# One tile for a raw weight piece and its block sums, and weight pools by stage, in a two-layer mLSTM and attention trunk

## The chip, the cores and the metric

The kernel runs on one core of a Trainium2 chip, in one launch. The metric is the device time in microseconds (us). Before the change the median of 3 runs is 2645.78 us (2642.27 to 2648.69).

## The reference

512 positions of width 2048 go through two layers, all in float32. Each layer normalises, scales and shifts its input by values computed from a condition vector c, and adds a gated branch to the residual stream. The first layer's branch is an mLSTM of 8 heads, the second's an attention of 16 heads in a band of chunks with a learned bias; the second reads keys and values computed from the residual stream after the first.

```
proj = h @ w_in                      # layer 1: 2048 -> q, k (8 x 256), v, o, z (8 x 512), gates
qk = silu(causal_conv(q, k))
ht = rmsnorm_per_head(mlstm(q, k, v, li, lf))
x  = x + gate * rmsnorm((sigmoid(o) * ht * silu(z)) @ w_out)

kv = modulate(rmsnorm(x)) @ kv_w     # keys and values, 2048 each
qz = h2 @ w_in                       # layer 2: q and z, 2048 each
o  = softmax(q k^T / sqrt(128) + bias, band) v
x  = x + gate * rmsnorm((o * silu(z)) @ w_out)
```

## The kernel before, in words

Every float32 product is made of three products of a faster form. `split` (line 244) makes two halves of a tile: ScalarE (ACT) casts it to the rounded form, `hi`, and VectorE (DVE) subtracts this from the source, `lo`. `mm3` issues hi x hi, hi x lo and lo x hi on TensorE (PE). All products have line 316.

Weights come in pieces. A piece is a raw tile `wr` of 128 x 1024 numbers (512 KB), loaded by a DMA on SyncE's queue (SP, line 260, `raw_load`) from a stream `wst` that lies in the order of use; `wpiece` splits it into the halves of a tile `wh`. Where a stage saves multiplications by sums of weight blocks (`proj_s` and `proj_v`: late heads, keys, attention's queries), `wpiece` first makes block sums: three DVE operations (lines 283, 284, 285) write a tile `ws` of 128 x 768, one of them over a block of the raw tile, and `ws` is split by a cast and a subtraction of its own into a tile `wsh`. PE uses `wh` and `wsh` in turn: of the four banks d, c, a, b of a product, d and b need `wh`, c needs `wsh`, a needs both.

One pool `wp`, opened at the start and never closed, holds the raw tiles (3 buffers) and the `wh` tiles (3 buffers). Tiles `ws` and `wsh` (2 buffers each) lie in pools of the stages. A tile of 2 x 1024 halves has 128 spare numbers, and the two halves start at offsets in it that `WIDE`, `STILL` and `MOVING` give by kind of stage.

The stages, in order: modulation sums (tiles `ada`, 1 MB loads of the condition's weights, summed on DVE at line 555) beside the products of head 0 and 1; head 2, whose v still uses whole weights; late heads 3 to 7 (q, k, v, o, z with block sums, 32 pieces each); the first layer's output projection (`ps_y`); values and keys; attention (16 heads of 4 pieces); the second output projection. Line 1301 copies values out of the banks, line 1302 stores them to a scratch `vsc`; line 1016 stores a head's gated output `zo` to the scratch `ysc`, from where the output projection loads it.

A scheduler sets the order on each engine. Each engine's queue is worked in order, SP's too: a load that waits holds up those behind it. Tiles of a pool that is opened where others lay wait, tile by tile, for the last use of what lay there (`reuse_waits="tile"`).

Of the kernel before, what the change touches and what calls it, by code (L numbers as in the profile page):

```python
# [9 lines left out]
F32 = mybir.dt.float32  # L10
F32R = mybir.dt.float32r
# [4 lines left out]
P = 128  # L16
D = 2048
S = 512
# [14 lines left out]
EXTW = 640  # L33
AHEAD = 300
RAW_BUFS = 3
SPARE = 128
WIDE, STILL, MOVING = (64, 0, 64, 1), (16, 0, 48, 1), (28, 0, 28, 1)

PAIRS = [(0, 1), (2, 3)]
BLOCKS = [(0, 2), (2, 6), (6, 12), (12, 16)]  # L40
# [149 lines left out]
def hybrid_trunk(ctx, tc, xT, xN, c, adaT, cols, wst, wg, ext, kc, out):  # L190
    nc = tc.nc
# [59 lines left out]
    loads = []  # L251
    pin = tc.keep_in_program_order

    def raw_load(keep=lambda ins: ins):

        i, at = wpos
        n = sum(w for _, _, w in order[i][1])
        wpos[:] = i + 1, at + P * n
        raw = wp.tile([P, 1024], F32, tag="raw", name=f"wr{i}", bufs=RAW_BUFS)[:, :n]
        keep(nc.sync.dma_start(raw, wst[at : at + P * n].rearrange("(p n) -> p n", p=P)))  # L260
        loads.append(raw)

    def wpiece(mat, groups=(), pl=None, bufs=(2, 2), early=False, at=WIDE):
# [8 lines left out]
        n = sum(w for _, _, w in blocks)  # L272
        with tc.high_priority(ahead[0]):
            if not loads:
                raw_load()
            raw = loads.pop(0)
            ts = []
            c0 = 0
            for j, ns in enumerate(groups):
                w = ns * P  # L280
                r = raw[:, c0 : c0 + 4 * w]
                t = pl.tile([P, 3 * w], F32, tag="ws", name=f"ws{i}_{j}", bufs=bufs[0])
                nc.vector.tensor_tensor(t[:, : 2 * w], r[:, w : 3 * w], r[:, : 2 * w], op=ALU.subtract)  # L283
                nc.vector.tensor_tensor(r[:, w : 2 * w], t[:, w : 2 * w], r[:, :w], op=ALU.add)  # L284
                nc.vector.tensor_tensor(t[:, 2 * w :], r[:, 3 * w :], r[:, w : 2 * w], op=ALU.subtract)  # L285
                ts.append(t)
# [12 lines left out]
            parted[:] = split(hi, lo, raw, *first[1:] if i < 3 else ())  # L299
            out = [(hi, lo)]  # L300
            for j, t in enumerate(ts):
                n = 3 * groups[j] * P
                parts = pl.tile([P, 2 * 768 + SPARE], F32R, tag="wsh", name=f"wsh{i}_{j}", bufs=bufs[1])
                sh, sl = halves(parts, at, n, 768)
                split(sh, sl, t)
                out.append((sh, sl))
        return out

    def halves(parts, at, n, w):
        (a, i), (b, j) = at[:2], at[2:]  # L310
        return parts[:, i * w + a : i * w + a + n], parts[:, j * w + b : j * w + b + n]

    product = [None]

# [48 lines left out]
    def proj_s(mat, xs, ss, f, z1, z2, name, pl, bufs, at={}, merged=False, banks="pppp"):  # L363

        D, C, A, B = [(newa if b == "a" else newp)(f"ps_{n}{name}") for n, b in zip("dcab", banks)]
        pieces = pair_pieces(f, merged)
        begun = set()
        h0, h1_ = slice(0, 256), slice(256, 512)  # L370
        for i, (sk, nk) in enumerate(pieces):
            if i in at:
                at[i]()
            main, *extra = wpiece(mat, [len(ks) for ks in sk], pl, bufs, at=STILL)

            def acc(ps, cols, parts, b, x, last):
                start = id(ps) not in begun
                begun.add(id(ps))
                w = slice(b * P, (b + 1) * P)
                mm3(ps[:, cols], parts[0][:, w], parts[1][:, w], x[:, 0, :], x[:, 1, :], start, last, 256)  # L380

            def eight():
                b0 = 4 * sum(len(ks) for ks in sk)
                for m, k in enumerate(nk):
                    for j in range(2):
                        for t, ps in enumerate((A, B)):
                            acc(ps, slice(0, S), main, b0 + 4 * m + 2 * j + t, xs[2 * k + j], False)

            def seven(g, ks):
                ns = len(ks)  # L390
                b0 = 4 * sum(len(u) for u in sk[:g])
                end = i == len(pieces) - 1 and g == len(sk) - 1
                for ps, cols, t, at_, x, last in (
                    (D, h1_, 0, 1, lambda k: ss[k][1], False),
                    (D, h0, 0, 0, lambda k: xs[2 * k][:, :, h0], end),
                    (C, h0, 1, 1, lambda k: ss[k][2], False),
                    (C, h1_, 1, 0, lambda k: ss[k][0], end),
                    (A, h0, 0, 3, lambda k: xs[2 * k + 1][:, :, h0], False),
                    (A, h1_, 1, 2, lambda k: xs[2 * k + 1][:, :, h1_], end),
                    (B, h0, 0, 2, lambda k: ss[k][3], end),  # L400
                ):
                    if i == 0 and g == 0 and ps is B:
                        eight()
                    for j, k in enumerate(ks):
                        acc(ps, cols, extra[g] if t else main, (0 if t else b0) + at_ * ns + j, x(k), last and j == ns - 1)

            if i:
                eight()
            for g, ks in enumerate(sk):
                seven(g, ks)  # L410
        with tc.high_priority(AHEAD):
            def z(t, half=None):
                return t.rearrange("p h (a t) -> p h a t", a=2) if half is None else like(t[:, half, :], 256)
# [12 lines left out]

    def proj_v(mat, xs, ss, zs, name, pl, bufs, at={}):
# [42 lines left out]
        for k in range(n):  # L470
            if k in at:
                at[k]()
            held.append((k, *wpiece(mat, [2], pl, bufs, at=MOVING)))
            if k in (0, n - 2):
                continue
            for b in range(2):
# [53 lines left out]
    phA = ExitStack()  # L530
    tp = phA.enter_context(pool("t1", bufs=3, side="right"))
# [347 lines left out]
    for h in range(NH):  # L879
# [180 lines left out]
    def y_tile(k):  # L1060
        while len(ys) <= k:
            n = len(ys)
            h, q = divmod(n // 2, 2)
            with tc.high_priority(AHEAD):
                if n < 4:
                    raw = wp.tile([P, 2, S], F32, tag="raw", name=f"yr{h}_{q}", bufs=RAW_BUFS)
# [470 lines left out]
    def y2_tile(k):  # L1537
        while len(y2) <= k:
            i = len(y2) // 2
            raw = wp.tile([P, 2, S], F32, tag="raw", name=f"y2r{i}", bufs=RAW_BUFS) if i < 2 else op.tile([P, 2, S], F32, tag="yr", name=f"y2r{i}", bufs=2)  # L1540
# [59 lines left out]
    finish(3)  # L1600
    assert wpos[0] == len(order)
    ost.close()


def layouts(x, c, ada_w, ada_b, g_pre, g_post, a_w_in, a_conv_w, a_conv_b, a_gate_b, a_g_head,
# [56 lines left out]
```

## Time and profile before

| what | value |
| --- | --- |
| median of 3 runs | 2645.78 us |
| the profiled execution | 2643.91 us |
| its span | 2642.1 us |
| PE busy | 2578.2 us (98%) |
| DVE busy | 2361.1 us (89%) |
| ACT busy | 1470.2 us (56%) |
| pieces of 512 KB | 506 |

A group's row names line, engine, operation and tiles, then the count, the busy time and the mean of one in ns, then the engine's idle time just before these instructions and who ended it. Successive instructions of one engine overlap by some 0.1 us in these records, so a sum of means lies a little above the time they take. The windows by stage are: 426 to 593 us head 2; 593 to 1420 the late heads, 167 us each; 1420 to 1830 the output projection and the inputs of keys and values; 1830 to 2090 keys and values; 2090 to 2460 attention; then the second output projection.

### The profile page before, as it was taken

Reading aid. Unit: us, or ns where it says so; the run is one execution under the profiler, and the core shown is the slowest. Engines: PE = TensorE matmul, PEld = TensorE weight load, DVE = VectorE, ACT = ScalarE, POOL = GpSimd, SP = SyncE. Lnnn points to the kernel's source line nnn. Section 1 sums busy time; section 2 is a strip of 40 time slices with the busy share of each in tenths; the row PEclk is TensorE's granted clock in tenths of the full one; section 3 lists DMA queues with packets and bytes.
Section 4 is the critical chain, followed back from the end, with each engine's and each line's share of the span. In section 5 each row is a group of like instructions: output and inputs, shape, how many; then the busy total and the mean of one; then the engine's idle time right before and its main releaser. Section 6 shows DMA issues by size and latency. Waiting matters only on the chain. (4 is left out here: it accounts for less than half of the span.)

```text
span 2642.1 us, 45681 instructions
## 1 busy us (share of the span) xinstructions
PE 2578.2 (98%) x17994; PEld 2405.8 (91%) x17994; DVE 2361.1 (89%) x3804; ACT 1470.2 (56%) x2128; POOL 30.5 (1%) x61
## 2 busy tenths in 40 slices
PE   8999999999999999999999999999999999999998
PEld 6887888899999999999999898788999899999887
DVE  8978999999999999999998886977997899999667
ACT  4344533466556566565666443578544876767523
POOL 0000010000000000000000000000000000000000
PEclk9999999999999999999999999999999999999999
DMA  9776798433333333333336648889754744444697
GB/s 365 310 266 244 261 360 297 171 112 123 106 119 106 121 119 114 107 113 125 109 121 224 211 152 300 307 261 308 236 173 143 234 134 143 132 137 134 226 315 251
DMA packets 157234, 514.71 MB, mean 195 GB/s; under 512 B 16805, under 2 KB 30661, under 8 KB 142553
## 3 DMA queue, kind: packets, MB, share of 16 engines
q1 hardware_dynamic: 148810, 452.02, 50.2%
q0 software_dynamic: 8208, 59.77, 6.1%
q8 instruction: 141, 2.31, 0.4%
q14 instruction: 75, 0.61, 0.1%
HBM read 478.11 MB, written 38.85 MB: 196 GB/s over the span
## 5 line engine op out<-in xcount | busy, mean ns | idle before, releaser
L244 ACT CAST wh<-wr 128x1024 fp32r<-128x1024 f32 (+1 forms) x536 | 552.6, 1032 | 481.2 <-DVE wr L284 99.4
L244 DVE TENSOR_TENSOR wh<-wr,wh 128x1024 fp32r<-128x1024 f32 (+1 forms) x536 | 642.9, 1202 | 112.3 <-ACT wh L244 111.4
L244 ACT CAST wsh<-ws 128x768 fp32r<-128x768 f32 (+1 forms) x296 | 242.3, 819 | 294.7 <-PE ps_az L316 60.8
L244 DVE TENSOR_TENSOR wsh<-ws,wsh 128x768 fp32r<-128x768 f32 (+1 forms) x296 | 276.3, 934 | 31.0 <-ACT wsh L244 30.0
L555 DVE CUSTOM_DVE_ANT_0 ada<-ada,scB,cl 128x2048 f32<-128x2048 f32 (+1 forms) x89 | 206.1, 2323 | 13.9 <-DMA ada<-in_adaT 13.9
L283 DVE TENSOR_TENSOR ws<-wr 128x512 f32<-128x512 f32 (+1 forms) x296 | 198.1, 673 | 4.7 <-DMA wr<-in_wst 4.3
L316 PE MATMUL ps_y<-wh,y 128*128 128x512 f32 x768 | 169.9, 381 | 3.7 <-ACT sqy L1116 2.3
L316 PE MATMUL ps_y_False<-wh,y 128*128 128x512 f32 x768 | 168.9, 380 | 2.4 <-DVE wh L244 2.3
L316 PEld LDWEIGHTS ps_y<-wh,y 128*128 128x128 f32 x768 | 143.8, 189 | 26.5 <-ACT sqy L1116 3.1
L316 PEld LDWEIGHTS ps_y_False<-wh,y 128*128 128x128 f32 x768 | 144.2, 189 | 24.9 <-DVE wh L244 4.6
L316 PE MATMUL ps_v<-wh,h 128*128 128x512 f32 x576 | 128.9, 383 | 0.0
L316 PE MATMUL ps_kv<-wh,hkv 128*128 128x512 f32 x576 | 126.8, 381 | 0.6 <-ACT hkv L244 0.5
L316 PEld LDWEIGHTS ps_v<-wh,h 128*128 128x128 f32 x576 | 109.3, 191 | 16.2 <-issue 0.9
L285 DVE TENSOR_TENSOR ws<-wr 128x256 f32<-128x256 f32 (+1 forms) x296 | 121.4, 414 | 2.8
L316 PEld LDWEIGHTS ps_kv<-wh,hkv 128*128 128x128 f32 x576 | 108.0, 189 | 17.1 <-ACT hkv L244 1.2
L284 DVE TENSOR_TENSOR wr<-ws,wr 128x256 f32<-128x256 f32 (+1 forms) x296 | 121.3, 413 | 2.4
L316 PE MATMUL ps_l<-h,wh 128*128 128x512 f32 x480 | 107.8, 380 | 2.7 <-DVE wh L244 2.1
L316 PEld LDWEIGHTS ps_l<-h,wh 128*128 128x128 f32 x480 | 90.2, 189 | 17.4 <-DVE wh L244 3.3
L316 PE MATMUL ps_azo<-h,wh 128*128 128x256 f32 (+1 forms) x606 | 93.0, 285 | 1.6 <-DVE e L865 1.6
L316 PE MATMUL ps_y_True<-wh,y 128*128 128x512 f32 x384 | 83.3, 379 | 0.0
L316 PEld LDWEIGHTS ps_azo<-h,wh 128*128 128x128 f32 x606 | 79.3, 192 | 2.8 <-issue 1.8
L316 PEld LDWEIGHTS ps_y_True<-wh,y 128*128 128x128 f32 x384 | 72.5, 189 | 10.2
(417 smaller groups left out, 5861.1 us busy)
## 6 DMA issues: line engine op xcount, KB each, us to landing
wr<-in_wst SPq DMA_DIRECT2D x506, 512.0 KB, 3.9
ada<-in_adaT POOLq DMA_DIRECT2D x57, 1024.0 KB, 7.3
ada<-in_adaT SPq DMA_DIRECT2D x49, 1024.0 KB, 7.0
ada<-in_adaT SPq DMA_DIRECT2D x36, 512.0 KB, 7.0
wr<-in_wst SPq DMA_DIRECT2D x26, 384.0 KB, 5.4
xt<-nsc SPq DMA_DIRECT2D x32, 256.0 KB, 4.4
yr<-ysc SPq DMA_DIRECT2D x28, 256.0 KB, 6.0
ysc<-zo SPq DMA_DIRECT2D x24, 256.0 KB, 4.4
```

Source lines behind the costliest of these rows:

```text
L244: ins = nc.scalar.copy(hi, src), nc.vector.tensor_tensor(lo, src, hi.bitcast(F32), op=ALU.subtract)
L283: nc.vector.tensor_tensor(t[:, : 2 * w], r[:, w : 3 * w], r[:, : 2 * w], op=ALU.subtract)
L284: nc.vector.tensor_tensor(r[:, w : 2 * w], t[:, w : 2 * w], r[:, :w], op=ALU.add)
L285: nc.vector.tensor_tensor(t[:, 2 * w :], r[:, 3 * w :], r[:, w : 2 * w], op=ALU.subtract)
L316: product[0] = nc.tensor.matmul(ps, a, b, start=start, stop=stop)
L555: pin(nc.vector.tensor_tensor_reduce(c, c, (sc or scB)[:, j * w : (j + 1) * w], 1.0, mod[:, i : i + 1] if j else col(CB + i), ALU.mult, AL ...
```

## The change

In two kinds of stage, called joint (from head 2's v through head 7, and attention), a raw tile is 1,792 wide. The block sums are written behind the raw numbers in the same tile, and one cast and one subtraction over up to 1,792 columns split both, into one tile of two halves of 1,792. Such a stage has 2 raw buffers. In the others the raw tile stays at 1,024 with 3 buffers, and `ws` and `wsh` stay apart. Spare numbers and offsets go everywhere.

Because the tile sizes differ by stage, the pool of the weights is closed and opened anew at four places: after the modulation sums (ahead of head 2's v), after head 7, ahead of attention, and ahead of the last output projection.

```
 RAW_BUFS = 3
-SPARE = 128
-WIDE, STILL, MOVING = (64, 0, 64, 1), (16, 0, 48, 1), (28, 0, 28, 1)
+JOINT = 1024 + 768
...
-    wp = ctx.enter_context(tc.tile_pool(name="wp", bufs=3, side="right"))
+    def weights_to(joint):
+
+        if store:
+            store.pop()[0].close()
+        st = ExitStack()
+        name = f"w{len(store_names)}"
+        store_names.append(name)
+        store.append((st, st.enter_context(pool(name, bufs=3, side="right")), joint))
...
+    def raw_tile(name):
+        _, wp, joint = store[0]
+        return wp.tile([P, JOINT if joint else 1024], F32, tag="raw", name=name, bufs=2 if joint else RAW_BUFS)
...
-                t = pl.tile([P, 3 * w], F32, tag="ws", name=f"ws{i}_{j}", bufs=bufs[0])
+                t = whole[:, c1 : c1 + 3 * w] if joint else pl.tile([P, 3 * w], F32, tag="ws", name=f"ws{i}_{j}", bufs=bufs[0])
...
-            parts = wp.tile([P, 2 * 1024 + SPARE], F32R, tag="parts", name=f"wh{i}")
-            hi, lo = halves(parts, at, n, 1024)
+            parts = wp.tile([P, 2, JOINT if joint else 1024], F32R, tag="parts", name=f"wh{i}")
+            if joint:
+                split(parts[:, 0, :c1], parts[:, 1, :c1], whole[:, :c1])
+                return [(parts[:, 0, a : a + w], parts[:, 1, a : a + w]) for a, w in [(0, n)] + [t[:2] for t in ts]]
+            hi, lo = parts[:, 0, :n], parts[:, 1, :n]
...
+    weights_to(False)
     mst = ExitStack()
...
             mst.close()
+            weights_to(True)
...
     hqst.close()
+    store.pop()[0].close()
     hst.close()
     phA.close()
+    weights_to(False)
...
     tst.close()
+    weights_to(True)
     at = ast.enter_context(pool("att"))
...
     ast.close()
+    weights_to(False)
     ost = ExitStack()
```

How the orders stand, at three places. DVE at head 2's v, before (`wr81` is the first raw piece of that v, `ada48` and so on the modulation's tiles):

```order
L244 TENSOR_TENSOR wh80_3361<-wr80_3359,wh80_3361 128x1024
L555 ISA ada48_0_3097,mod_102<-ada48_0_3097,scB_122,cl_99 128x2048
L555 ISA mod_102 128x1
L244 TENSOR_TENSOR qk_2_1_3244<-cv_2_1_3236,qk_2_1_3244 128x512
L244 TENSOR_TENSOR wh81_3422<-wr81_3420,wh81_3422 128x1024
L798 SCALAR_TENSOR_TENSOR cv_2_2_3312<-cu_2_2_3313,cl_99,cv_2_2_3312 128x511
L555 ISA ada49_0_3099,mod_102<-ada49_0_3099,scB_122,cl_99 128x2048
```

and in the changed kernel, 40 rows later in the queue:

```order
L254 TENSOR_TENSOR h1s0_3_3463<-h1r0_0_3453,h1s0_3_3463 128x256
L254 TENSOR_TENSOR h1s0_42_3466<-h1r0_1_3455,h1s0_42_3466 128x512
L254 TENSOR_TENSOR h1s1_3_3537<-h1r1_0_3527,h1s1_3_3537 128x256
L853 TENSOR_TENSOR h1r1_1_3529<-h1_3_448 128x512
L521 TENSOR_TENSOR h1r1_0_3527<-h1r1_0_3527,h1r1_1_3529 128x256
L524 TENSOR_TENSOR h1r1_1_3529<-h1r1_1_3529,h1r1_0_3527 128x256
L525 TENSOR_TENSOR h1r1_1_3529<-h1r1_1_3529 128x256
L254 TENSOR_TENSOR wh81_3426<-wr81_3424,wh81_3426 128x1024
```

The subtraction of piece 81 stood right behind `ada48`; now it stands behind `ada55`, `ada56` and the sums of h (`h1s`). Raw tile 81 now lies where an `ada` tile lay, and its load waits for the sum of `ada55`.

SP ahead of the first output projection, before (`wr265` is its first piece, `yr0_0` its first input); the stores of head 7's `zo7` come 28 rows later:

```order
L260 DMA wr265_14998<-in_wst 128x1024
L1067 DMA yr0_0_15003<-ysc_72 128x1024
L260 DMA wr266_15037<-in_wst 128x1024
L1067 DMA yr0_1_15042<-ysc_72 128x1024
L260 DMA wr267_15088<-in_wst 128x1024
L260 DMA wr268_15144<-in_wst 128x1024
```

and in the changed kernel:

```order
L563 DMA ada57_0_14300<-in_adaT 128x2048
L1122 DMA ssum_107<-ggd_77 128x512
L1031 DMA ysc_72<-zo7_0_0_13319 128x512
L1031 DMA ysc_72<-zo7_1_0_13535 128x512
L1031 DMA ysc_72<-zo7_2_0_13751 128x512
L274 DMA wr265_14302<-in_wst 128x1024
L1084 DMA yr0_0_14307<-ysc_72 128x1024
L274 DMA wr266_14341<-in_wst 128x1024
```

The load of piece 265 now stands behind three of the four stores of head 7's output.

SP ahead of attention, before (`wr433` is the queries' first piece, `h2r` their inputs, `vsc3` the store of the last values):

```order
L1386 DMA h2r2_21686<-nsc_75 128x512
L1386 DMA h2r3_21690<-nsc_75 128x512
L260 DMA wr433_21792<-in_wst 128x1024
L1386 DMA h2r4_21699<-nsc_75 128x512
L1386 DMA h2r5_21703<-nsc_75 128x512
L260 DMA wr434_21846<-in_wst 128x1024
L1386 DMA h2r6_21712<-nsc_75 128x512
```

and in the changed kernel:

```order
L1403 DMA h2r15_21072<-nsc_75 128x512
L1319 DMA vsc3_90<-v3_0_20966 512x1x128 x2
L1319 DMA vsc3_90<-v3_2_20971 512x1x128 x2
L1425 DMA kt0_21092<-ksc0_79 128x512
L1425 DMA vt0_21200<-vsc0_87 128x512
L274 DMA wr433_21100<-in_wst 128x1024
L274 DMA wr434_21150<-in_wst 128x1024
```

Loads 433 to 436 stood among the loads of `h2r`, ahead of the stores of the values; now they stand behind all of them, and load 433 waits for the four stores.

More of the change, by code (lines that the diff above doesn't have):

```diff
@@ L201, in pool @@
         return tc.tile_pool(name=name, bufs=bufs, reuse_waits="tile", **kw)
-    wp = ctx.enter_context(tc.tile_pool(name="wp", bufs=3, side="right"))
+    phA = ExitStack()
+    tp = phA.enter_context(pool("t1", bufs=3, side="right"))
+    store, store_names = [], []
+    def weights_to(joint):
[5 more added lines that the diff above has]
+        store.append((st, st.enter_context(pool(name, bufs=3, side="right")), joint))
     ysc = dram.tile([NH, P, 4, S], F32, name="ysc")
@@ L258, in raw_load, with wpiece @@
         wpos[:] = i + 1, at + P * n
-        raw = wp.tile([P, 1024], F32, tag="raw", name=f"wr{i}", bufs=RAW_BUFS)[:, :n]
-        keep(nc.sync.dma_start(raw, wst[at : at + P * n].rearrange("(p n) -> p n", p=P)))
+        raw = raw_tile(f"wr{i}")
+        keep(nc.sync.dma_start(raw[:, :n], wst[at : at + P * n].rearrange("(p n) -> p n", p=P)))
         loads.append(raw)
-    def wpiece(mat, groups=(), pl=None, bufs=(2, 2), early=False, at=WIDE):
+    def wpiece(mat, groups=(), pl=None, bufs=(2, 2), early=False):
         if stock and not early:
@@ L272, in wpiece @@
         n = sum(w for _, _, w in blocks)
+        _, wp, joint = store[0]
         with tc.high_priority(ahead[0]):
@@ L275, in wpiece @@
                 raw_load()
-            raw = loads.pop(0)
+            whole = loads.pop(0)
+            raw = whole[:, :n]
             ts = []
-            c0 = 0
+            c0, c1 = 0, n
             for j, ns in enumerate(groups):
@@ L285, in wpiece @@
                 nc.vector.tensor_tensor(t[:, 2 * w :], r[:, 3 * w :], r[:, w : 2 * w], op=ALU.subtract)
-                ts.append(t)
+                ts.append((c1, 3 * w, t))
                 c0 += 4 * w
-            parts = wp.tile([P, 2 * 1024 + SPARE], F32R, tag="parts", name=f"wh{i}")
-            hi, lo = halves(parts, at, n, 1024)
+                c1 += 3 * w
+            parts = wp.tile([P, 2, JOINT if joint else 1024], F32R, tag="parts", name=f"wh{i}")
[3 more added lines that the diff above has]
+            hi, lo = parts[:, 0, :n], parts[:, 1, :n]
             if i == 0:
@@ L300, in wpiece @@
             out = [(hi, lo)]
[L301 to L304, printed above, removed]
+            for j, (_, w, t) in enumerate(ts):
+                parts = pl.tile([P, 2, 768], F32R, tag="wsh", name=f"wsh{i}_{j}", bufs=bufs[1])
+                sh, sl = parts[:, 0, :w], parts[:, 1, :w]
                 split(sh, sl, t)
@@ L307, in wpiece @@
         return out
-    def halves(parts, at, n, w):
-        (a, i), (b, j) = at[:2], at[2:]
-        return parts[:, i * w + a : i * w + a + n], parts[:, j * w + b : j * w + b + n]
     product = [None]
@@ L373, in proj_s @@
                 at[i]()
-            main, *extra = wpiece(mat, [len(ks) for ks in sk], pl, bufs, at=STILL)
+            main, *extra = wpiece(mat, [len(ks) for ks in sk], pl, bufs)
             def acc(ps, cols, parts, b, x, last):
@@ L472, in proj_v @@
                 at[k]()
-            held.append((k, *wpiece(mat, [2], pl, bufs, at=MOVING)))
+            held.append((k, *wpiece(mat, [2], pl, bufs)))
             if k in (0, n - 2):
@@ L527, in modulated @@
         return a, b, nc.vector.scalar_tensor_tensor(lo, tmp, shift, hi.bitcast(F32), op0=ALU.add, op1=ALU.subtract)
-    phA = ExitStack()
-    tp = phA.enter_context(pool("t1", bufs=3, side="right"))
+    weights_to(False)
     mst = ExitStack()
@@ L1065, in y_tile @@
                 if n < 4:
-                    raw = wp.tile([P, 2, S], F32, tag="raw", name=f"yr{h}_{q}", bufs=RAW_BUFS)
+                    raw = raw_tile(f"yr{h}_{q}")[:, :1024].rearrange("p (a t) -> p a t", a=2)
                     nc.sync.dma_start(raw, ysc[h, :, 2 * q : 2 * q + 2, :])
@@ L1539, in y2_tile @@
             i = len(y2) // 2
-            raw = wp.tile([P, 2, S], F32, tag="raw", name=f"y2r{i}", bufs=RAW_BUFS) if i < 2 else op.tile([P, 2, S], F32, tag="yr", name=f"y2r{i}", bufs=2)
+            raw = raw_tile(f"y2r{i}")[:, :1024].rearrange("p (a t) -> p a t", a=2) if i < 2 else op.tile([P, 2, S], F32, tag="yr", name=f"y2r{i}", bufs=2)
             with tc.high_priority(AHEAD):
@@ L1602, in hybrid_trunk @@
     ost.close()
+    store.pop()[0].close()
 def layouts(x, c, ada_w, ada_b, g_pre, g_post, a_w_in, a_conv_w, a_conv_b, a_gate_b, a_g_head,
```

## Prediction

> **What bounds the kernel now.** I read the page's head first, then the windows by stage, the waits of PE by stage, the groups by form, and at last the timelines at the four places where the change opens a new weight pool.
>
> ```profile
> span 2642.1 us, 45681 instructions
> PE 2578.2 (98%) x17994; PEld 2405.8 (91%) x17994; DVE 2361.1 (89%) x3804; ACT 1470.2 (56%) x2128; POOL 30.5 (1%) x61
> ```
>
> PE is busy for all but 64 us of the span. A change that relieves DVE and ACT can win back only idle time of PE; a change that makes PE wait pays in full. The windows say where that idle time lies (columns: length, then PE, PEld, DVE, ACT, POOL busy, clock, DMA share, GB/s):
>
> ```profile
> 426.00:593.00 167.00, 162.95 (x992) 149.00 (x990) 163.63 (x270) 87.22 (x127) 5.31 (x10) 1.00 0.49 172
> 593.00:760.00 167.00, 163.44 (x1416) 161.61 (x1417) 159.30 (x262) 101.72 (x129) 0.00 (x0) 1.00 0.36 116
> 1420.00:1560.00 140.00, 139.87 (x871) 128.90 (x870) 123.34 (x196) 66.59 (x99) 0.00 (x0) 1.00 0.59 202
> 2090.00:2460.00 370.00, 368.10 (x3134) 362.77 (x3134) 350.15 (x763) 260.41 (x446) 0.00 (x0) 1.00 0.48 147
> 2460.00:2642.00 182.00, 169.98 (x793) 145.71 (x791) 122.42 (x181) 62.43 (x104) 0.00 (x0) 0.99 0.77 261
> ```
>
> The second row is one late head (head 3; heads 4 to 7 read alike): PE idles 3.6 of 167 us although DVE is busy 95%. Attention idles 1.9 of 370. So the joint split has at most 5 x 3.6 + 1.9 = 20 us to win. What PE waits for in head 3, and in the window of head 2:
>
> ```profile
> PE ps_cv L316 <- DVE wsh L244: 2.1, 2, 1.2
> PE ps_n L316 <- DVE zo L1004: 1.3, 1, 1.3
> ...
> PE ps_azo L316 <- DVE e L865: 1.6, 1, 1.6
> PE ps_bzo L316 <- DVE p L870: 1.1, 1, 1.1
> ```
>
> **The joint split, by piece.** Groups by form (busy, mean ns; idle before):
>
> ```profile
> L244 DVE TENSOR_TENSOR wh<-wr,wh 128x1024 fp32r<-128x1024 f32 x506 | 616.6, 1220 | 108.5 <-ACT wh L244 107.7
> L244 DVE TENSOR_TENSOR wsh<-ws,wsh 128x768 fp32r<-128x768 f32 x283 | 269.2, 951 | 31.0 <-ACT wsh L244 30.0
> L555 DVE CUSTOM_DVE_ANT_0 ada<-ada,scB,cl 128x2048 f32<-128x2048 f32 x87 | 203.5, 2347 | 13.9 <-DMA ada<-in_adaT 13.9
> L283 DVE TENSOR_TENSOR ws<-wr 128x512 f32<-128x512 f32 x283 | 192.7, 684 | 4.5 <-DMA wr<-in_wst 4.1
> L285 DVE TENSOR_TENSOR ws<-wr 128x256 f32<-128x256 f32 x283 | 117.8, 420 | 2.8
> L284 DVE TENSOR_TENSOR wr<-ws,wr 128x256 f32<-128x256 f32 x283 | 117.6, 419 | 2.4
> L1013 DVE RECIPROCAL dd<-dd 128x512 f32<-128x512 f32 x8 | 26.8, 3346 | 0.7 <-ACT dd L1012 0.7
> ...
> L244 ACT CAST wh<-wr 128x1024 fp32r<-128x1024 f32 x506 | 529.5, 1046 | 464.8 <-DVE wr L284 99.4 <-DMA wr<-in_wst 77.7 <-PE ps_y L316 65.4
> L244 ACT CAST wsh<-ws 128x768 fp32r<-128x768 f32 x283 | 235.7, 833 | 294.4 <-PE ps_az L316 60.8 <-issue 51.1 <-PE ps_azo L316 40.0
> ```
>
> The subtraction grows by (1220 - 951)/256 = 1.05 ns an element, so one of 1,792 takes 1220 + 768 x 1.05 = 2027 ns instead of 2171: 0.144 us less. The same on ACT: 1046 + 768 x 0.832 = 1685 instead of 1879, 0.194 us less. The orders of the two kernels differ by 240 subtractions and 240 casts: DVE is 35 us less busy, ACT 47 us, all beside PE.
>
> The price is order and buffers. A joint piece must have its sums (0.684 + 0.420 + 0.419 = 1.52 us) before its cast, and its whole subtraction before any product. And a raw piece now has two buffers, not three, held from its load until the joint subtraction is done. The load:
>
> ```profile
> wr<-in_wst SPq DMA_DIRECT2D x32, 512.0 KB, 3.3
> ```
>
> That is head 3's; the life of a buffer is at least 3.3 + 1.52 + 1.69 + 2.03 = 8.5 us. With two buffers worked one behind the other (sums A, sums B, subtraction A, subtraction B), a cycle of two pieces is 3.3 until B's load lands behind its last subtraction, then B's sums 1.52, then 2 x 2.03: 8.9 us, in which DVE idles 8.9 - 2 x 3.55 = 1.8. A late head has 32 pieces, 16 such pairs, and DVE's other work: 159.3 - 32 x 3.69 = 41 us, 2.6 a pair. If that work fills the whole idle time, a pair takes 9.7 us; if none of it, 11.5. PE needs 163.4/16 = 10.2. So a head may take 163.4 (3.6 better than now) up to 16 x 11.5 = 184 (17 worse). The middle, 10.6, makes 169.6; I take 168.6, a little under it, because that other work is mostly of short steps, which fit into gaps: +1.6 a head, +8 for five. Attention likewise: 370/16 = 23.1 us a head in these windows, two pairs, so 17.8 + other work of 350.15/16 - 4 x 3.69 = 7.1, less up to 3.6 that fits in: 21.3 to 24.9. I take +0.25 a head, +4; ends -2 and +28. The Trainium skill, "Trainium Kernel Development and Optimization", section "Best Practices", asks for double buffers so that a load overlaps the work: by it two raw buffers are enough, no ring binds, and the sum below would be 61.6 - 20 = 42 us over now instead of 74. The cycle of 8.9 us above, in which the load lies open because sums and subtraction hold the same buffer, is why I don't go by it.
>
> **Spare bytes.** The halves lose their offsets. Groups of one shape with different stationary and moving tiles:
>
> ```profile
> L316 PE MATMUL ps_czo<-h1s,wsh 128*128 128x256 f32 x546 | 76.9, 275 | 0.2 <-DVE wsh L244 0.2
> ...
> L316 PE MATMUL ps_cv<-wsh,h1s 128*128 128x256 f32 x240 | 42.5, 279 | 10.6 <-DVE wsh L244 10.6
> ```
>
> These have different offsets and lie within 4 ns. I take 0; the ends are 4 ns x 17994 = 72 us either way, which I hold for very unlikely.
>
> **The four new pools.** This is the main term. Before, one pool held the weights throughout, and the first pieces of a stage were loaded and split while the stage before ran. Now each new pool's tiles lie where other tiles lay, and SP's and DVE's orders put the first load behind those tiles' last use.
>
> 1. Head 2's v. Before:
>
> ```profile
> 453.35 1.23 DVE L244 TENSOR_TENSOR wh<-wr,wh 128x1024 fp32r<-128x1024 f32 x1
> ...
> 478.43 2.35 DVE L555 CUSTOM_DVE_ANT_0 ada<-ada,scB,cl 128x2048 f32<-128x2048 f32 x1
> 480.70 1.22 DVE L244 TENSOR_TENSOR wh<-wr,wh 128x1024 fp32r<-128x1024 f32 x1
> ...
> 460.82 3.40 PE L316 MATMUL ps_v<-wh,h 128*128 128x512 f32 x15
> ```
>
> The first row is the split of piece 81, seven us ahead of its product (last row). After, load 81 waits for the sum of ada55, the one that starts at 478.43 here. Five subtractions (81 to 85, 1.14 us start to start) leave that stretch and some 1.5 us of h1 sums enter: the sum ends at 476.5 to 480. Behind it DVE has 7.9 us of ada56 and h1 sums before the subtraction of piece 81, which ends at about 486.5. PE does 18 products of the scores earlier (2.9 us), so it idles from 463.7 to 486.5: 22.8. What head 2 waits for now (1.6 + 1.1 + 0.2) goes. A long gap costs more than itself:
>
> ```profile
> 409.65 2.01 PE L316 MATMUL ps_n<-p,v 128*128 128x512 f32 x11 [1.51 <-ACT dd L991]
> 415.14 3.51 PE L316 MATMUL ps_n<-p,v 128*128 128x512 f32 x11 [3.49 <-DVE so L1004]
> ...
> 412.00:416.00 4.00, 0.86 (x2) 0.77 (x3) 4.00 (x6) 0.22 (x1) 0.48 (x1) 0.85 0.98 313
> 416.00:420.00 4.00, 4.00 (x18) 3.62 (x18) 2.81 (x6) 1.49 (x3) 0.00 (x0) 0.72 0.97 402
> ```
>
> After 3.5 us of idleness the granted clock falls below 1: (0.15 + 0.28) x 4 us = 1.7 us lost. Sum: 22.8 - 2.9 + 1.7 = +21.6. The Trainium skill, "TensorE: Matmul & The Clock Gate", section "HAM oscillation — how this bites in real kernels", tells of a kernel that ran 1.67 us at half clock behind each gap over 3.4 us; by it each gap here would cost 0.8 us more, not 1.7, and three of them 2.6 us less than I take. The rows above decide.
>
> 2. The first output projection.
>
> ```profile
> 1422.30 7.12 PE L316 MATMUL ps_n<-p,v 128*128 128x512 f32 x44
> 1429.14 10.63 PE L316 MATMUL ps_y_True<-wh,y 128*128 128x512 f32 x48
> ...
> 1440.67 0.68 DVE L1004 TENSOR_TENSOR zo<-ps_n,zo 128x512 f32<-128x512 f32 x1
> ...
> 1429.10 0.60 ACT L1003 ACTIVATE sq<-ps_n 128x512 f32<-128x512 f32 x1
> ```
>
> PE goes from head 7's ps_n to ps_y without a gap. After, load 265 stands on SP behind the stores of zo7_0 to zo7_2, so behind head 7's end: from 1429.1 the square (0.60), its sum, cast and subtraction (0.68, 0.60, 0.68), ps_q (about 0.7), two vector steps (0.68 each at most) and the root (0.6), the reciprocal (3.35), three products (0.68 each): 10.6. Then the load (3.9 in the row below), cast 1.05, subtraction 1.22, y's own first split (0.7) and some hand-over: about 18 us; with 1.7 for the clock, +19.7.
>
> 3. Attention.
>
> ```profile
> wr<-in_wst SPq DMA_DIRECT2D x506, 512.0 KB, 3.9
> vsc<-v SPq DMA_DIRECT2D x16, 256.0 KB, 3.4
> ...
> 2083.81 0.83 PE L316 MATMUL ps_dz<-h2s,wh 128*128 128x256 f32 x6
> ```
>
> Before, the queries start right behind the last values at 2083.81. After, load 433 waits until the stores of those values have landed: the last copy and its issue behind two ACT steps (about 1.9), landing 3.4, load 3.6 (between 3.3 and 3.9), sums 1.52, cast 1.69, subtraction 2.03: 14.1; +1.7 for the clock: +15.8. If piece 434's sums go first, 1.5 more.
>
> 4. Output.
>
> ```profile
> 2454.46 2.19 PE L316 MATMUL ps_y<-wh,y 128*128 128x512 f32 x9
> ```
>
> Before, ps_y fills the gaps of attention's tail from 2454.46. After, load 497 waits for the last query product: 3.9 + 1.05 + 1.22 = 6.2 us, part of it beside the tail's own products. I take +4.5, ends 2 and 8.
>
> Sum: 21.6 + 19.7 + 15.8 + 4.5 = 61.6, + 8 + 4 = 73.6 on the profiled execution's 2643.9 (span 2642.1, 1.8 around it): 2717.5; the median lies 1.9 above that execution: 2719 us.
>
> **Rivals.** (a) The forecast: the pools' openings cost 50 to 70, the rings -10 to +35. 2680 to 2765. Chance 0.84. (b) The ring of two sets the pace: DVE's other work fits nowhere into the idle times. Heads +17 x 5 = 85, attention +28, openings 61.6: 2643.9 + 175 = 2819. For it: DVE is 95% busy, and a reciprocal (3.35) can stand ahead of a subtraction. Against: three buffers have PE waiting 3.6 us a head only. Chance 0.11. (c) Faster. DVE's relief comes through and PE waits no more in late heads and attention: -20; this needs openings that cost under 20, so that the loads of the first pieces get free space at once and do not wait where the order puts them. 2624 to 2643; it decides at openings = 20. Against: the stores of zo7 stand ahead of load 265 in SP's own order, which alone is 18. Chance 0.02. (d) Openings and relief cancel: within 5.3 us, 0.2%, which is what a measurement of this kernel can tell from no change. Chance 0.03.
>
> **Numbers.** The likeliest is (a), 2719. The range 2680 to 2765 leaves out (c), (d), most of (b) and a little of (a). Faster 0.02, same 0.03, slower 0.95.
>
> **What would show it.** PE idle for about 20 us ahead of the first ps_v of head 2, 18 ahead of ps_y_True, 14 ahead of ps_dz, each with a clock under 1 behind it. A joint subtraction of 2.03 and a cast of 1.69 us. Late heads of 165 to 172 us, with PE's waits there on DVE wh. Wrong: gaps under 10 us at these places, or late heads above 175.

## The result and the profile after

The changed kernel takes 2820.99 us (median of 5 runs, 2816.72 to 2828.3), before it 2646.04 us (5 runs). The ratio is 1.0665, 95% interval 1.0644 to 1.0687: 175 us slower. The forecast was 2719 us, 2680 to 2765; slower was right, the size was not.

The head of the page after:

```profile
span 2815.0 us, 44877 instructions
PE 2630.1 (93%) x17994; PEld 2436.7 (87%) x17994; DVE 2366.0 (84%) x3564; ACT 1431.2 (51%) x1878; POOL 30.6 (1%) x61
```

PE now idles 185 us instead of 64 and is busy 52 us longer for the same 17994 products: its granted clock is lower (0.978 as a mean, 0.998 before). The operations themselves came out as costed, by form:

```profile
L254 DVE TENSOR_TENSOR wh<-wr,wh 128x1792 fp32r<-128x1792 f32 x230 | 462.2, 2021 | 48.7 <-ACT wh L254 48.3
...
L299 DVE TENSOR_TENSOR wr<-wr 128x512 f32<-128x512 f32 x230 | 158.2, 688 | 96.2 <-DMA wr<-in_wst 95.4
```

The joint subtraction takes 2021 ns (forecast 2027), the joint cast 1693 (forecast 1685). The second row is the new thing: ahead of the first block sum DVE idles 96 us for weight loads, where it idled 4.5 before (the row of L283 in the prediction).

DVE's busy time did not fall by the 35 us of the forecast, though: it is 2366.0 us, 2361.1 before (ACT's fell by 39, forecast 47). By the means, 230 joint subtractions do save 230 x (1221 + 953 - 2021) ns = 35 us. But successive instructions overlap a little, and busy time counts an overlap once: the means of head 3's DVE instructions before add up to 177.8 us with 159.3 busy, those of head 4 after to 171.1 with 156.4. Fewer instructions overlap less, so that busy time falls by less than the means do.

The 173 us by which the span grew, by stage. Stages are cut at the first product of each kind on PE's timelines; late heads run from the first ps_dzq of head 3 to the last ps_bzo of head 7, attention from the first ps_dz to the last ps_bz.

| stage | before, us | after, us | more |
| --- | --- | --- | --- |
| gap ahead of head 2's v | 0.2 | 23.1 | 22.9 |
| rest of head 2 | 130.0 | 138.8 | 8.8 |
| late heads | 830.9 | 900.9 | 70.0 |
| last ps_bzo to first ps_y_True | 7.4 | 25.7 | 18.3 |
| first output projection, keys and values | 654.5 | 657.0 | 2.5 |
| gap ahead of attention | 0.2 | 16.9 | 16.7 |
| attention | 369.6 | 393.4 | 23.8 |
| last ps_bz to first ps_y | 1.0 | 11.2 | 10.2 |
| last projection | 187.7 | 187.7 | 0.0 |

Each stage time here and below is of one profiled execution. Those of before and nospare (below), whose times are the same, differ by at most 1.2 us in late heads and attention. One execution of a kernel below, sep, took 7129 us, its three others 2770 to 2777; it is in sep's median and not in its ratio, and sep's stages are read from a second profile (sep_look).

The four openings of pools cost 68 us (forecast 61.6), one by one 22.9, 18.3, 16.7 and 10.2 (forecast 21.6, 19.7, 15.8 and 4.5). The two sums don't hold quite the same: these intervals leave out the clock lost behind them, for which the forecast had 1.7 us at each of the first three, and the first one holds 18 products of the scores, so that PE idles 17.4 of its 23.1 us. PE's timeline at three of them, the idle time ahead of each row in brackets:

```profile
470.19 3.25 PE L331 MATMUL ps_s<-qk,qk 128*128 128x512 f32 x9 [7.20 <-ACT qk L254]
483.38 1.22 PE L331 MATMUL ps_v<-wh,h 128*128 128x512 f32 x2 [9.94 <-ACT wh L254]
486.30 33.99 PE L331 MATMUL ps_v<-wh,h 128*128 128x512 f32 x144 [1.70 <-DVE wh L254]
...
1548.81 3.78 PE L331 MATMUL ps_y_True<-wh,y 128*128 128x512 f32 x8 [14.66 <-ACT y L254]
...
2222.59 0.80 PE L331 MATMUL ps_dz<-h2s,wh 128*128 128x256 f32 x2 [16.49 <-ACT wh L254]
```

The gaps lie where the prediction put them. What it missed is between the openings. Late heads and attention after (windows; columns as before):

```profile
802.10:985.00 182.90, 169.10 (x1418) 164.93 (x1418) 156.42 (x226) 93.41 (x94) 0.00 (x0) 0.98 0.31 102
...
2222.60:2612.60 390.00, 372.13 (x3116) 363.00 (x3117) 341.73 (x678) 239.70 (x356) 0.00 (x0) 0.99 0.39 122
```

A late head takes 182.9 us instead of 167. What PE and DVE waited for in this one (head 4), below the dots DVE's largest wait in head 4 before:

```profile
PE ps_dzo L331 <- DVE wh L254: 4.8, 6, 1.6
PE ps_dv L331 <- DVE wh L254: 3.9, 3, 2.2
PE ps_s L331 <- DVE e L879: 2.8, 1, 2.8
...
DVE wr L299 <- DMA wr<-in_wst: 12.4, 9, 2.5
DVE wh L254 <- ACT wh L254: 9.2, 8, 1.9
...
DVE wsh L244 <- ACT wsh L244: 2.9, 4, 1.0
```

PE waits for the joint subtraction, and DVE for loads and casts: the ring of load, sums, cast and subtraction holds them up. The five late heads together, before and after (windows):

```profile
590.90:1421.80 830.90, 812.92 (x7059) 803.95 (x7058) 789.41 (x1286) 506.60 (x641) 0.00 (x0) 1.00 0.35 116
...
622.20:1523.10 900.90, 837.15 (x7038) 818.53 (x7037) 779.90 (x1117) 464.92 (x461) 0.00 (x0) 0.98 0.32 105
```

Of the 70 us, 46 are idle time of PE (18.0 us before, 63.7 after). The other 24 are longer busy time for the same products, at a mean granted clock of 0.98 instead of 1.00. How much of those 24 the ring would have taken anyway isn't shown. In attention PE waits for something else, below the dots what DVE waited for in attention before:

```profile
PE ps_t L1481 <- DVE s L1472: 15.9, 28, 1.2
...
DVE wr L299 <- DMA wr<-in_wst: 27.2, 33, 2.6
DVE wh L254 <- ACT wh L254: 14.7, 17, 1.0
...
DVE wsh L244 <- ACT wsh L244: 13.8, 13, 1.1
DVE ws L283 <- DMA wr<-in_wst: 0.8, 1, 0.8
```

It waits for the softmax's last step on DVE (s, line 1472), not for weights; and DVE loses 42 us to loads and casts meanwhile, 27 of them to loads, which had cost it 0.8.

### The profile page after: what moved, and what is told of

Its sections match the earlier page's. It is cut to its first block, busy times and chain, and to the rows that moved or that the text cites. A ratio compares the mean times of both kernels' runs of the same rounds, so it can differ in the third digit from the quotient of the medians.

```text
span 2815.0 us, 44877 instructions
## 1 busy us (share of the span) xinstructions
PE 2630.1 (93%) x17994; PEld 2436.7 (87%) x17994; DVE 2366.0 (84%) x3564; ACT 1431.2 (51%) x1878; POOL 30.6 (1%) x61
## 4 chain that ended last, share of the span: by engine, by line
PE 22%; DVE 17%; DMA 11%; ACT 4%; issue 3%; SPq 0%; DVEq 0%; ACTq 0%
DVE wh L254 8%; DMA wr<-in_wst 8%; PE ps_y_True L331 3%; PE ps_y_False L331 3%; ACT wh L254 3%; PE ps_y L331 2%; DMA ada<-in_adaT 2%; PE ps_kv L331 2%; DVE wr L299 2%; PE ps_ak L331 2%; PE ps_ck L331 1%; PE ps_dk L331 1%; DMA xt<-nsc 1%; PE ps_bk L331 1%; DVE wr L300 1%
## 5 line engine op out<-in xcount | busy, mean ns | idle before, releaser
L254 ACT CAST wh<-wr 128x1024 fp32r<-128x1024 f32 (+3 forms) x536 | 702.9, 1316 | 789.0 <-DVE wr L301 254.9
L254 DVE TENSOR_TENSOR wh<-wr,wh 128x1024 fp32r<-128x1024 f32 (+3 forms) x536 | 828.9, 1554 | 185.7 <-ACT wh L254 184.8
L299 DVE TENSOR_TENSOR wr<-wr 128x512 f32<-128x512 f32 (+1 forms) x240 | 162.4, 677 | 105.6 <-DMA wr<-in_wst 104.8
L331 PE MATMUL ps_azo<-h,wh 128*128 128x256 f32 (+1 forms) x1152 | 155.5, 280 | 0.0
L331 PEld LDWEIGHTS ps_azo<-h,wh 128*128 128x128 f32 x1152 | 141.1, 192 | 1.1
L331 PEld LDWEIGHTS ps_v<-wh,h 128*128 128x128 f32 x576 | 110.2, 193 | 29.2 <-ACT wh L254 10.2
L331 PE MATMUL ps_dzo<-h1s,wh 128*128 128x256 f32 x546 | 87.3, 283 | 21.9 <-DVE wh L254 21.1
L300 DVE TENSOR_TENSOR wr<-wr 128x256 f32<-128x256 f32 (+1 forms) x240 | 99.4, 415 | 3.3
L301 DVE TENSOR_TENSOR wr<-wr 128x256 f32<-128x256 f32 (+1 forms) x240 | 99.5, 416 | 3.0
L331 PEld LDWEIGHTS ps_dzo<-h1s,wh 128*128 128x128 f32 x546 | 72.1, 191 | 30.6 <-DVE wh L254 28.7
L331 PE MATMUL ps_az<-h,wh 128*128 128x256 f32 x768 | 96.7, 275 | 0.0
```

Of the source, the lines that this page charges most:

```text
L254: ins = nc.scalar.copy(hi, src), nc.vector.tensor_tensor(lo, src, hi.bitcast(F32), op=ALU.subtract)
L331: product[0] = nc.tensor.matmul(ps, a, b, start=start, stop=stop)
```

## The experiments

All late-head and attention times below are cut as in the table above. For the start there were two theories. The ring theory: two raw buffers, held from the load until the joint subtraction is done, set the pace. The rival, the joint-split theory: PE waits because a whole piece must be cast and subtracted before its first product, whatever the buffers. The times of attnonly, pools_p2, sep_r3p2 and attsep_r5p2 are of one execution each.

| kernel | us | late heads | attention |
| --- | --- | --- | --- |
| before | 2646 | 830.9 | 369.6 |
| the change | 2821 | 900.9 | 393.4 |
| pools | 2687 | 830.0 | 367.9 |
| pools_r2 | 2701 | 841.5 | 369.0 |
| pools_p2 | 2700 | 837.9 | 368.4 |
| sep | 2777 | 870.6 | 380.4 |
| r3p2 | 2761 | 844.0 | 390.7 |
| sep_r3p2 | 2727 | 833.0 | 379.6 |
| r3p2_ord | 2739 | 848.4 | 367.4 |
| attnonly | 2720 | 829.9 | 389.7 |
| attr3 | 2716 | 829.9 | 385.3 |
| attsep_r3 | 2708 | 830.0 | 382.0 |
| attr5p2 | 2720 | 829.9 | 387.9 |
| attsep_r5p2 | 2709 | 829.9 | 379.1 |
| attr3_ord | 2697 | 830.0 | 368.1 |

### The openings and the spare bytes

pools, against the changed kernel (the first pair of lines is at head 2, the second at attention):

```
-            weights_to(True)
+            weights_to(False)
...
-    weights_to(True)
+    weights_to(False)
```

> The changed kernel with no stage joint: raw tiles of 1024 with 3 buffers, separate casts, but the weight pools are still closed and opened at the four places, and the spare numbers are gone. Both theories: late heads 166 to 169 us each, attention 366 to 374, the four openings at their cost in the changed kernel, some 66 us in all: 2705 to 2725 us. If the openings cost only because the joint tiles are larger, 2650 to 2680.

It took 2686.8 us, ratio 1.0158 (1.014 to 1.0175): 41 us over before, less than expected, with late heads and attention as before. The gaps: 3.0 us ahead of head 2's v, 25.5 to ps_y_True, 12.7 ahead of attention, 11.2 ahead of the last projection. At the first, PE idles 4.3 us more four products later.

nospare, against before:

```
-SPARE = 128
-WIDE, STILL, MOVING = (64, 0, 64, 1), (16, 0, 48, 1), (28, 0, 28, 1)
+SPARE = 0
+WIDE, STILL, MOVING = (0, 0, 0, 1), (0, 0, 0, 1), (0, 0, 0, 1)
```

> The kernel before without the spare numbers and offsets, and nothing else. Both theories: no difference, within 0.2% of before (2640 to 2651 us). If the offsets keep TensorE or the two other engines out of each other's way: 2660 or more, with longer matrix products in the same stages.

Ratio 1.0002 (0.9993 to 1.0011): the spare bytes are worth nothing that can be measured. This kernel has one pool and no spare bytes, pools has the same tiles in reopened pools: the 41 us between them are the openings alone. The other 20 us of the first opening come with the joint tiles: the gap is 3.2 us in attnonly, which has no joint tile there, and 23.1 in the change. There the first raw tile falls on the place of a late ada tile: its load starts at 477.71 us, when the sum over that tile ends.

### Late heads: buffers, and how long one is held

r3p2, against the changed kernel (the tiles of halves go from three to two as the raw tiles go from two to three, so two things change at once):

```
-... bufs=3, side="right")), joint))
+... bufs=2 if joint else 3, side="right")), joint))
...
-... bufs=2 if joint else RAW_BUFS)
+... bufs=3 if joint else RAW_BUFS)
```

> The changed kernel with 3 raw buffers and 2 tiles of halves in the joint stages (2 and 3 in the change). Ring theory (two raw buffers set the pace): late heads fall from 180 us to 167 to 172 each, attention from 390 to 370 to 376, DVE's waits for the weights' loads there go; the openings stay at some 66 over before; in all 2720 to 2745 us. Rival, joint-split theory (PE waits because a whole joint piece must be cast and subtracted before its first product): late heads stay at 178 to 182, in all 2810 to 2830.

It took 2761.25 us, ratio 1.0438 (1.0419 to 1.0458). Late heads fell from 900.9 to 844.0, which the ring theory had said; attention stayed near the change (390.7), which it hadn't. DVE's waits in head 4 here:

```profile
DVE wh L254 <- ACT wh L254: 7.9, 10, 1.5
DVE wr L299 <- DMA wr<-in_wst: 4.3, 5, 1.2
```

The wait for loads fell from 12.4 to 4.3 us.

sep, against the changed kernel (the same with an execution more for the profile is sep_look):

```
-                split(parts[:, 0, :c1], parts[:, 1, :c1], whole[:, :c1])
+                split(parts[:, 0, :n], parts[:, 1, :n], whole[:, :n])
+                if c1 > n:
+                    split(parts[:, 0, n:c1], parts[:, 1, n:c1], whole[:, n:c1])
```

> The changed kernel, but raw numbers and block sums, still in one tile with two raw buffers, are split by two casts and two subtractions, as before the change. Ring theory: a buffer is held as long as now (until the second subtraction), so late heads stay at 178 to 186 us, in all 2810 to 2860. Joint-split theory: PE gets the first part as early as before, late heads come back to 167 to 171, in all 2740 to 2760.

> The kernel of sep again, for its profile by stage; its time is known, 2777 us, between what both theories had. If the ring holds it up, late heads stay above 175 us and attention falls to 370 to 375 (two shorter subtractions let the softmax's steps through). If the joint split holds up PE in late heads, they are at 167 to 171 and attention stays at 390.

It took 2776.89 us, ratio 1.0488 (1.0466 to 1.051), between the two theories, neither of which had it: late heads at 870.6 are 40 us over before with separate splits and two buffers, and the joint operation adds 30 more.

pools_r2, against pools, has two raw buffers of 1,024 in head 2 to 7 and in attention:

```
-... bufs=2 if joint else RAW_BUFS)
+... bufs=2 if len(store_names) in (2, 4) else RAW_BUFS)
```

> The kernel of pools (no joint stage) with 2 raw buffers of 1024 instead of 3 in the stages that the change makes joint: the ring alone. A buffer is held 3.3 + 1.52 + 1.05 + 1.22 = 7.1 us instead of 8.5. Ring theory: late heads 169 to 176 us, attention 370 to 378, in all 2705 to 2740. If two buffers cost nothing by themselves: late heads 167, in all 2685 to 2692.

It took 2701.1 us, ratio 1.0206 (1.0192 to 1.022): 168.3 us a late head, a little less than the ring theory had said, and attention at 369.0, where it had said 370 to 378. Two buffers that are free again after the first subtraction cost late heads 11 us; two that are held until the last one cost 40 (sep); two held through a joint cast and subtraction cost 71. So late heads follow the ring theory in this form: how many buffers there are, and how long each is held. The rival has a share: the joint operation by itself costs late heads 11 us even with three buffers (844.0 in r3p2, 833.0 in sep_r3p2 below, which differ in nothing else), so that not all of the last 30 us need come of the longer hold.

pools_p2 (pools with two tiles of halves) and sep_r3p2 (r3p2 with separate splits) ask what the last 13 us of r3p2 are:

```
-... bufs=3, side="right")), joint))
+... bufs=2 if name in ("w1", "w3") else 3, side="right")), joint))
```

> The kernel of pools (no joint stage) with 2 tiles of halves instead of 3 in the stages that the change makes joint. If what r3p2 keeps over before (2.6 us a late head, 21 in attention) comes of its two tiles of halves, late heads are at 168 to 171 and attention at 375 to 390 here; if it comes of the joint split, late heads are at 167 and attention at 368.

> The kernel of r3p2 (3 raw buffers, 2 tiles of halves in all joint stages) with separate splits. Ring theory: late heads as in r3p2 or up to 2 us a head less (167 to 171), since with three buffers the time that one is held matters little. Joint-split theory: the joint split's delay is what is left of r3p2's 2.6 us a head over before, so late heads are at 166.5 to 167.5.

Late heads took 837.9 and 833.0; the second, 166.6 us a head, is what the joint-split theory had said. Two tiles of halves cost 8 without a joint tile, and a joint tile with separate splits 2 to 3, hardly more than two profiles differ: with three raw buffers, what is left comes of the joint operation together with two tiles of halves. These two were not told apart further.

### Attention: the ring theory falls

attnonly, against the changed kernel (at head 2):

```
-            weights_to(True)
+            weights_to(False)
```

> The changed kernel with the joint split in attention alone; head 2's v through head 7 have raw tiles of 1024 with 3 buffers. Both theories: late heads 166 to 169 us, attention as in the change (388 to 392), openings as in the change; 2725 to 2755 us. If attention is slow because of what late heads leave behind, attention falls to 370 and the time to 2720.

It took 2719.89 us, less than expected, because the first opening fell by 20 us as well; late heads 829.9, attention 389.7. What slows attention is in attention. attr3 is attnonly with three raw buffers, attsep_r3 the same with separate splits:

> The kernel of attnonly with 3 raw buffers in attention instead of 2 (and 3 tiles of halves, as there). Ring theory for attention: DVE waits no more for the weights' loads, attention falls from 390 to 368 to 374, in all 2695 to 2705 us. Rival, order theory (the joint subtraction of 2 us stands ahead of the softmax's steps in DVE's queue, whatever the buffers): attention stays at 384 to 391, in all 2712 to 2722.

> The kernel of attr3 (joint tile in attention alone, 3 raw buffers) with two casts and two subtractions in place of the joint ones. Attention took 385 there, 380 with two raw buffers and separate splits, 368 without a joint tile. If both the long subtraction and the two buffers hold up the softmax's steps in DVE's queue: attention 368 to 374, in all 2692 to 2705 us. If the shared tile itself costs (sums written into the raw tile, which stays held), attention stays at 378 to 385, in all 2705 to 2718.

Attention took 385.3 and 382.0 (2716.38 us, ratio 1.0277, 1.0256 to 1.0298; and 2708.46 us, ratio 1.0237, 1.0214 to 1.026). A third buffer, which had given late heads 57 us (with one tile of halves less), gave attention 4. To be sure of it, five raw buffers and two tiles of halves, with the joint split and with separate ones:

```
-... bufs=2 if joint else RAW_BUFS)
+... bufs=5 if joint else RAW_BUFS)
```

> The kernel of attnonly (joint tile and joint split in attention alone) with 5 raw buffers and 2 tiles of halves; two tiles of halves alone cost attention nothing (pools_p2: 368). Attention took 390 with 2 raw buffers, 385 with 3. Ring theory (a raw tile is held until its last subtraction, which the order puts late, and 3 buffers are still too few): DVE's waits for the loads go, attention falls to 368 to 374, in all 2690 to 2702 us. Order theory (the long subtraction ahead of the softmax's steps, and sums written into the raw tile, whatever the buffers): attention stays at 380 to 388, in all 2705 to 2720.

> The same with separate casts and subtractions (attsep_r3 with 5 raw buffers and 2 tiles of halves). Ring theory: attention 368 to 371, 0 to 4 us under attr5p2. Order theory: attention 376 to 383, as with 2 and 3 raw buffers.

387.9 and 379.1: the ring theory is wrong for attention (attr5p2: 2719.69 us, ratio 1.0277, 1.0259 to 1.0294). Separate splits are faster there each time, by 3 us with three buffers and by 9 with five, so the length of the joint operation has a share. But DVE waited for loads even so; in attr5p2:

```profile
DVE wr L299 <- DMA wr<-in_wst: 30.9, 33, 2.5
DVE s L1468 <- PE ps_s L331: 5.8, 10, 2.0
```

With five buffers one would expect no load to be late. DVE's timeline shows what it stood waiting for, with the softmax's steps right behind, PE's what that cost, and SP's, in the first row, when the load went out:

```profile
2308.94 0.33 SPq L274 DMA_DIRECT2D wr<-in_wst  x1
...
2306.89 2.02 DVE L254 TENSOR_TENSOR wh<-wr,wh 128x1792 fp32r<-128x1792 f32 x1
...
2313.66 0.69 DVE L299 TENSOR_TENSOR wr<-wr 128x512 f32<-128x512 f32 x1 [2.29 <-DMA wr<-in_wst]
2314.27 0.42 DVE L1468 CUSTOM_DVE_ANT_0 s<-ps_s,bias 128x256 f32<-128x256 f32 x1
...
2315.43 2.02 DVE L254 TENSOR_TENSOR wh<-wr,wh 128x1792 fp32r<-128x1792 f32 x1
2317.36 0.22 DVE L1471 RECIPROCAL mx<-mx 128x1 f32<-128x1 f32 x2
...
2318.22 1.09 PE L1481 MATMUL ps_t<-kcs,s 128*128 128x128 f32 x6 [0.68 <-DVE s L1472]
```

In the order, the sum at 2313.66 is that of the piece four ahead of the one whose subtraction comes next. Before, a sum needed a `ws` tile, of which there were two, so it could run two pieces ahead at most, and its load had landed by then (DVE waited for one load in all of attention, 0.8 us). Now it needs nothing but its load. The order makes it as soon as the load is due, with any number of buffers: the load goes out at 2308.94, when the subtraction of the piece five before has just given up its buffer, and the sum stands waiting for it 2.29 us. DVE works in order, so the softmax waits as well.

attr3_ord and r3p2_ord put that limit back as an order, against attr3 and r3p2:

```
...
-                nc.vector.tensor_tensor(t[:, : 2 * w], r[:, w : 3 * w], r[:, : 2 * w], op=ALU.subtract)
+                head = nc.vector.tensor_tensor(t[:, : 2 * w], r[:, w : 3 * w], r[:, : 2 * w], op=ALU.subtract)
+                if joint and len(subs) > 1:
+                    behind(head, subs[-2])
...
-                split(parts[:, 0, :c1], parts[:, 1, :c1], whole[:, :c1])
+                subs.append(split(parts[:, 0, :c1], parts[:, 1, :c1], whole[:, :c1])[0])
```

> The kernel of attr3 (joint in attention alone, 3 raw buffers, attention 385 us) with one constraint on DVE's order more: the sums of a piece stand behind the joint subtraction of the piece two before. The ring theory has fallen for attention (5 buffers: 388). New theory, sums run ahead: since the sums now need no tile of their own, the order makes them as soon as a load has landed, so that DVE, which works in order, stands waiting for loads with the softmax's steps behind it, with any number of buffers. By it DVE's wait for loads (30 us) goes and attention falls to 368 to 375, in all 2690 to 2704 us. Rival, the long subtraction: it still stands ahead of the softmax's steps, attention stays at 382 to 388.

> The kernel of r3p2 (all joint stages with 3 raw buffers and 2 tiles of halves; late heads 168 to 173 us, attention 391) with the same constraint. Sums-run-ahead theory: attention 368 to 376, late heads 165 to 169, in all 2725 to 2740 us. Rival: attention 385 to 391, late heads unchanged, 2755 to 2765.

attr3_ord took 2697.2 us, ratio 1.019 (1.0175 to 1.0205), r3p2_ord 2739.03, ratio 1.0345 (1.0328 to 1.0362). Attention is at 368.1 and 367.4 us, with the joint split in it. What DVE still waits for there in attr3_ord:

```profile
DVE s L1470 <- PE ps_s L333: 13.8, 16, 3.4
DVE wh L254 <- ACT wh L254: 7.0, 21, 0.6
```

No wait for a load is left, and none of PE for s. So what slowed attention is shown: the sums that ran ahead. With them held back the long subtraction costs nothing that shows. Late heads did not gain (848.4, 844.0 in r3p2), where 165 to 169 us a head was expected; the cause stays open. With the change's two buffers this order should not help, since a load then starts only after the subtraction of the piece two before, right where the sums would wait; no run shows it.

No kernel here beats the one before. The joint split at its best has attention at 367.4 to 368.1 us, as pools has it without a joint tile (367.9): it wins nothing that can be measured, and the reopened pools cost 41 us.

## Why the prediction was wrong

- **What bounds the kernel**: right in that less work on DVE and ACT had little to win; pools and attr3_ord show attention at the same 368 us without and with the joint split. The relief was taken too large for DVE, 35 us by the means, where its busy time in the late heads fell by 9.5 and in all rose by 5.
- **The four openings**: right in place, and nearly in size: 61.6 us forecast, 68.1 measured. The last was mis-sized (4.5 forecast, 8 as its upper end, 10.2 measured): PE has a gap of 3.33 us there that waits for the softmax's end, and which ps_y filled before. It is the opening's own, since pools, with attention as before, has it too (3.34 us, the same 11.2 in all). The clock behind the long gaps was taken too small (below).
- **Spare bytes at nothing**: right (nospare).
- **Late heads, "I take 168.6, a little under it"**: this step failed. The term was +8 for five heads and came out at +70: a head takes 180 to 183 us. What was mis-sized is DVE's other work, "41 us, 2.6 a pair". The 159.3 us in its sum are busy time, in which successive instructions overlap; the 32 x 3.69 taken off add means, in which they don't. By means alone the other work is 177.8 - 118 = some 60 us. As time it is an estimated 52.5, with the overlap of (177.8 - 159.3)/262 = 0.07 us taken off for each of its 102 instructions: 3.3 us a pair. With that the two ends are 10.4 and 12.2 us a pair, and their middle, 11.3, makes some 180 us a head. How much of that work fits into gaps was judged about rightly: DVE waits 12.4 us for loads in head 4, of 16 x 1.8 = 29 if nothing fitted. But it waits 9.2 us for casts too, which the cycle leaves out. That the middle of the corrected ends lies so near the measured time is luck in part, since neither these casts nor PE's clock are in it. Attention's 7.1 us of other work come of the same mixed difference.
- **Attention, "+0.25 a head, +4"**: this step failed too: +23.8, inside its bounds (-2 to +28), but not by the ring from which they were worked out. The sums had lost the tile that kept them from running ahead, which the diff shows and the prediction does not price. Put back as an order, that limit brings attention to 368.1 us (attr3_ord); two raw buffers alone cost it 1 us (pools_r2).
- **Rest of head 2**: priced only by the 2.9 us of waits that were to go; it came out at +8.8. From the last ps_v to head 3 it takes 85.2 us before, 91.7 in the change, 92.9 in r3p2 (joint, three buffers), 92.3 in sep_look (separate, two) and 84.1 in sep_r3p2 (separate, three): either the joint operation or two buffers are enough for it.
- **The clock**: taken into account at the openings alone. Late heads lose to it as well, and it has a part in the 24 us by which PE is busy longer there.

Rival (b), 2819 us with a chance of 0.11, came out in its number. In late heads the ring did set the pace, as it says, though not because nothing fits in; for attention its mechanism is wrong. That the number fits within 2 us is luck: late heads came out 15 us under its 85 and attention 4 under its 28, the openings 6.5 over its 61.6, and the rest of head 2, which it leaves out, took 8.8.

## What to carry to other kernels

A merged operation that saves time on an engine that is not the bottleneck was worth nothing here, and what it holds was worth much: count the buffers and the time that each is held, from the load to the last read. When an engine's other work is worked out as a difference, take means on both sides or busy times on both: mixed, they made it a fifth too small here. A tile that looks like waste can be what keeps an operation from running ahead; when it goes, look in the order for what now stands at the head of a queue waiting for a transfer. Closing and opening a pool between stages cost 10 to 18 us at three of the four places here even with the same tiles, 3 at the other, and 20 more there where a larger tile fell on one in late use.

## What was not expected of the hardware

The clock fell behind gaps well under the 3.5 us from which the prediction took its price. In head 4 after, PE's timeline and the windows there:

```profile
843.10 0.38 PE L331 MATMUL ps_dv<-wh,h1s 128*128 128x256 f32 x1 [0.71 <-ACT wh L254]
844.40 0.38 PE L331 MATMUL ps_av<-wh,h 128*128 128x256 f32 x1 [0.37 <-DVE zq L436]
847.01 0.79 PE L331 MATMUL ps_dv<-wh,h1s 128*128 128x256 f32 x2 [2.23 <-DVE wh L254]
884.74 1.65 PE L331 MATMUL ps_s<-qk,qk 128*128 128x256 f32 x6 [2.78 <-DVE e L879]
...
846.00:850.00 4.00, 2.99 (x14) 2.99 (x15) 4.00 (x4) 3.67 (x4) 0.00 (x0) 0.59 0.40 131
882.00:886.00 4.00, 1.26 (x6) 1.26 (x7) 3.73 (x8) 1.97 (x2) 0.00 (x0) 0.78 0.39 138
886.00:890.00 4.00, 4.00 (x30) 4.00 (x30) 2.84 (x4) 0.80 (x3) 0.00 (x0) 0.79 0.09 15
```

A gap of 2.23 us with two short ones ahead of it, and one of 2.78 us by itself, each cost some 1.7 us of clock: 0.41 x 4 = 1.6, and (0.22 + 0.21) x 4 = 1.7. That is 3.4 of the 16 us that this head lost. What length of gap is enough isn't settled by these rows; the next longest gaps of this head, 1.57 and 1.37 us, left the clock at 1.00.

The long gaps cost more than the prediction's 1.7 us. Behind the 16.49 us ahead of attention the granted clock is 0.50 from 2222 to 2226 us, with PE busy for 3.30, and 0.61 from 2226 to 2230: 0.50 x 3.30 + 0.39 x 4 = 3.2 us.
